# A third of the low weights made by a ScalarE copy and an adding DMA

## The chip, the core and the metric

The kernel runs on one core of a Trainium2 chip. A core has five engines that run side by side, each in the order of its own instruction stream: TensorE (PE in the profile, its weight loads PEld), VectorE (DVE), ScalarE (ACT), GpSimd (POOL) and SyncE (SP), which here only issues DMAs. Engines and DMAs wait for each other by semaphores. The metric is the device time of one execution in microseconds; the time of a kernel is the median of its runs.

## The reference

One layer of a hybrid encoder, for one batch of 256 tokens of width 2048, in float32:

```python
n = rms_norm(h, norm_mix_w[l])
u = n @ w_in[l]
...
mixed = jax.nn.sigmoid(g_attn) * attn_out + jax.nn.sigmoid(g_ssd) * ssd_out
h = h + mixed @ w_out[l]
h = h + conv_ffn(rms_norm(h, norm_ffn_w[l]), ...)
return rms_norm(h, norm_final_w)
```

`attn_out` is a multi-head latent attention with 16 heads, `ssd_out` a chunked state-space scan in both directions with 64 heads in 8 groups, `conv_ffn` a gated MLP of width 5632 with a short convolution. Nearly all the arithmetic lies in products of the 256 tokens with large weight matrices.

## The kernel before

**Split numbers.** The matrix products run in a reduced-precision form of float32 (`F32R`). To keep accuracy, every operand is cut into a high part (the value as rounded to that form) and a low part (the value less its high part), and a product is made of three: high by high, high by low, low by high. The weights come from HBM as float32 and are split on the chip.

**Slabs and halves.** All weights are cut into slabs of 128 x 16 x 128 numbers (1 MB). The list `jobs` holds one entry per slab, in the order in which TensorE multiplies them. A slab lies in one of three `raw` buffers (`RAWB=3`), loaded by SP in `load` (L131 and L133). A slab has two halves, and the list `halves` holds them all: 670, of which 654 have eight blocks of 128 columns and 16, the last ones of the short slabs of `w_dn`, have four. The very first slab is multiplied unsplit and has none.

**The split.** `split_to` takes the halves in order; `hptr[0]` counts them. Each half gets a high buffer `wh` and a low buffer `wl` out of five of each (`HB=5`). ScalarE copies the raw half into `wh` with rounding (L150), and VectorE subtracts the high part from the raw half into `wl` (L151). In the main loop, before the matmuls of half n are emitted, `split_to(n + HB)` emits the split of the halves up to n + 4. The split of half n + 4 takes the buffers that half n - 1 used, so ScalarE waits there for TensorE's last matmul of half n - 1, and TensorE needs the result four halves later. The next load into a `raw` buffer waits for the last reader of that buffer's second half.

**Kinds of jobs.** A dense job (`dense`) multiplies a block of weights `wh` with high and low activations side by side (512 columns, L176) and `wl` with the high activations (256 columns, L177), eight times per half; the last slab of a run uses three matmuls instead (`mm3`, L156 to L158). A quad job (`quad`) has four smaller loads and the weights as the moving side (L204 to L206); it serves the branch gates and the two output projections of the branches. 160 halves belong to quad jobs.

**Stages.** By the trace: latents and the attention up to about 370 us, with quad slabs of the gates and of the attention's output projection in between; the SSD branch from about 395 to 880 us in eight head groups; its output projection, all quad, from 950 to 1126; `w_out` up to 1217; then the FFN up to 1957 in three parts, each an up-projection (`w_up`) with a convolution followed by a down-projection (`w_dn`). In the SSD stage ScalarE and VectorE also carry the convolutions (L672, L675, L676), the decays (`ssd_decay`, L721 to L727) and the scaling of the score blocks (`ssd_p`, L747, L748).

**What sets the order.** The opening block (weights of the first two halves and the first activations) is emitted under `tc.manual_schedule()` and keeps its order. For the rest a planner orders each engine's instructions, with priority in the order of emission; the semaphores follow from which instruction reads and writes which buffer. SP's queue holds nearly all loads in order; ScalarE's queue issues a few small DMAs; GpSimd's queue issues none.

## Time and profile before

| | |
|---|---|
| Median of 3 runs | 1975.71 us (1975.28 to 1976.85) |
| Profiled execution | 1974.66 us |
| Its span, first to last instruction | 1972.9 us |
| TensorE busy | 1956.5 us, 99% |
| VectorE busy | 1466.5 us, 74% |
| ScalarE busy | 1208.5 us, 61% |
| GpSimd busy | 0.2 us |
| DMA traffic | 379.32 MB, mean 192 GB/s |
| Granted TensorE clock, mean | 0.998 |

The page lists the busy time of each engine, the chain of work that ended last, the costliest groups of instructions by line, and the DMA issues. A group row gives line, engine, operation, the tiles it writes and reads, its shape and count, then its busy time, the mean of one in ns, and the engine's idle time just before, with what ended that. A row of waits reads: who waited, for what, us in total, times, longest. A timeline row gives the start in us from the span's begin, the duration, the instruction and, in brackets, the idle time before it and what ended it. A row of a stretch gives its length and each engine's busy time, with counts in brackets. A DMA issue row gives what is written and read, the queue, the count, the size of one and the median time from issue to landing.

### The profile page before, as it was taken

To read this page: it belongs to the slowest core of one execution; us is meant where nothing else is said; L and a number is where in the kernel's file an instruction comes from. 1 tells how busy PE (TensorE), PEld (TensorE's weight loads), DVE (VectorE), ACT (ScalarE), POOL (GpSimd) and SP (SyncE) were. 2 spreads that over 40 slices of the span, in tenths; PEclk is the share of its full clock that TensorE was granted. 3 is DMA by queue.
4 is the path that set the end of the run, shared out by engine and by line. 5 is a ranking of instruction groups with operands and counts; after the bars stand their busy time and mean duration, and the time that the engine had idled before them with its cause. 6 is when DMAs were issued, how large, how long until landed. Compare 5 with 4: busy or idle time off the path is not lost.

```text
span 1972.9 us, 29057 instructions
## 1 busy us (share of the span) xinstructions
PE 1956.5 (99%) x11136; PEld 1702.4 (86%) x11136; DVE 1466.5 (74%) x2349; ACT 1208.5 (61%) x1892; POOL 0.2 (0%) x4
## 2 busy tenths in 40 slices
PE   9999999999999999999999999999999999999997
PEld 8899988888888888888888888888888888888886
DVE  7997745779887988888455576888657777557776
ACT  6666544688988898786444455555435555345564
POOL 0000000000000000000000000000000000000000
PEclk9999999999999999999999999999999999999999
DMA  7554456666466556645766565555555555555553
GB/s 289 166 175 157 137 180 225 230 214 220 165 215 214 204 180 220 221 158 173 229 198 200 199 219 192 188 188 186 185 192 186 180 190 192 179 185 192 187 161 123
DMA packets 93260, 379.32 MB, mean 192 GB/s; under 512 B 10688, under 2 KB 11328, under 8 KB 62912
## 3 DMA queue, kind: packets, MB, share of 16 engines
q1 hardware_dynamic: 91440, 375.09, 56.2%
q10 hardware_dynamic: 1680, 2.37, 0.4%
q8 instruction: 87, 1.43, 0.3%
q14 instruction: 53, 0.43, 0.1%
HBM read 371.91 MB, written 4.33 MB: 191 GB/s over the span
## 4 chain that ended last, share of the span: by engine, by line
PE 93%; DVE 3%; ACT 2%; issue 1%; DMA 1%; SPq 0%; DVEq 0%; ACTq 0%
PE g L176 41%; PE g L177 21%; PE g L204 7%; PE g L206 7%; PE g L205 7%; PE g L158 1%; PE g L157 1%; PE g L156 1%; DVE wl L151 1%; ACT wh L150 1%; PE s L780 1%; PE s L157 0%; PE s L789 0%; DVE bcf L675 0%; PE s L158 0%
## 5 line engine op out<-in xcount | busy, mean ns | idle before, releaser
L151 DVE TENSOR_TENSOR wl<-raw,wh 128x1024 fp32r<-128x1024 f32 (+1 forms) x670 | 809.3, 1212 | 393.9 <-ACT wh L150 381.5
L150 ACT ACTIVATE wh<-raw 128x1024 fp32r<-128x1024 f32 (+1 forms) x670 | 700.3, 1048 | 647.8 <-PE g L176 433.1
L176 PE MATMUL g<-xHL,wh 128*128 128x512 f32 x1424 | 503.7, 398 | 2.0 <-DVE cu L229 2.0
L176 PE MATMUL g<-hHL,wh 128*128 128x512 f32 x1360 | 477.6, 396 | 0.0
L177 PE MATMUL g<-xHL,wl 128*128 128x256 f32 x1424 | 399.8, 281 | 0.8 <-DVE wl L151 0.8
L177 PE MATMUL g<-hHL,wl 128*128 128x256 f32 x1360 | 381.6, 281 | 0.0
L176 PEld LDWEIGHTS g<-xHL,wh 128*128 128x128 f32 x1424 | 267.3, 188 | 65.7 <-issue 1.2
L176 PEld LDWEIGHTS g<-hHL,wh 128*128 128x128 f32 x1360 | 255.1, 188 | 60.8
L177 PEld LDWEIGHTS g<-xHL,wl 128*128 128x128 f32 x1424 | 269.1, 189 | 1.5 <-DVE wl L151 1.1
L177 PEld LDWEIGHTS g<-hHL,wl 128*128 128x128 f32 x1360 | 257.0, 189 | 0.0
L176 PE MATMUL g<-aHL,wh 128*128 128x512 f32 x692 | 243.7, 398 | 0.0
L177 PE MATMUL g<-aHL,wl 128*128 128x256 f32 x692 | 193.2, 280 | 0.0
L176 PEld LDWEIGHTS g<-aHL,wh 128*128 128x128 f32 x692 | 130.0, 188 | 32.1 <-DVE aHL L919 0.7
L177 PEld LDWEIGHTS g<-aHL,wl 128*128 128x128 f32 x692 | 130.5, 189 | 0.1
L204 PE MATMUL g<-wh,xHL 128*128 128x512 f32 x256 | 100.1, 392 | 0.0
L204 PE MATMUL g<-wh,yHL 128*128 128x512 f32 x256 | 99.8, 390 | 0.0
L206 PE MATMUL g<-wh,xHL 128*128 128x512 f32 x256 | 99.8, 390 | 0.0
L205 PE MATMUL g<-wl,xHL 128*128 128x512 f32 x256 | 99.8, 390 | 0.0
L206 PE MATMUL g<-wh,yHL 128*128 128x512 f32 x256 | 99.6, 389 | 0.0
L205 PE MATMUL g<-wl,yHL 128*128 128x512 f32 x256 | 99.6, 389 | 0.0
L901 DVE SCALAR_TENSOR_TENSOR uc<-u,V,uc 128x255 f32<-128x255 f32 x176 | 84.7, 481 | 4.6 <-ACT uc L899 1.5
L176 PE MATMUL g<-mHL,wh 128*128 128x512 f32 x240 | 83.6, 392 | 0.0
(298 smaller groups left out, 2603.5 us busy)
## 6 DMA issues: line engine op xcount, KB each, us to landing
raw<-in_w_in SPq DMA_DIRECT2D x88, 1024.0 KB, 4.9
raw<-in_w_up SPq DMA_DIRECT2D x88, 1024.0 KB, 4.9
raw<-in_w_in SPq DMA_DIRECT2D x128, 256.0 KB, 4.0
raw<-in_w_os SPq DMA_DIRECT2D x128, 256.0 KB, 3.5
raw<-in_w_dn SPq DMA_DIRECT2D x32, 1024.0 KB, 4.9
raw<-in_w_oa SPq DMA_DIRECT2D x64, 256.0 KB, 3.8
FB<-acsD SPq DMA_DIRECT2D x32, 512.0 KB, 7.5
raw<-in_w_out SPq DMA_DIRECT2D x14, 1024.0 KB, 4.9
```

The lines of the kernel that those rows point to most:

```text
L150: act.activation(vh, r, AF.Copy)
L151: dve.tensor_sub(vl, r, f32(vh))
L156: pe.matmul(ps, lhsT=wH, rhs=xH, start=first, stop=False)
L157: pe.matmul(ps, lhsT=wH, rhs=xL, start=False, stop=False)
L158: pe.matmul(ps, lhsT=wL, rhs=xH, start=False, stop=last)
L176: pe.matmul(ps, lhsT=wh[:, b, :], rhs=x, start=k == 0, stop=False)
L177: pe.matmul(ps[:, 0, :], lhsT=wl[:, b, :], rhs=x[:, 0, :], start=False, stop=k == ktot - 1)
L204: pe.matmul(ps, lhsT=x[:, 0, ts], rhs=wH[:, kk, :], start=k == 0, stop=False)
L205: pe.matmul(ps, lhsT=x[:, 0, ts], rhs=wL[:, kk, :], start=False, stop=False)
L206: pe.matmul(ps, lhsT=x[:, 1, ts], rhs=wH[:, kk, :], start=False, stop=k == kt - 1)
L780: pe.matmul(px[j0][:, b, c * P:(c + 1) * P], lhsT=q.xw[:, 1 - c, js], rhs=q.cX[:, 1 - c, :], start=True, stop=True)
L901: dve.scalar_tensor_tensor(o[:, a], u[:, b], vcol("fcw", k * 88 + cb), o[:, a], ALU.mult, ALU.add)
```

## The change

Every third half (`hptr[0] % 3 == 2`), if it has eight blocks and isn't of a quad job, gets its low part in another way: ScalarE copies the raw half a second time, scaled by -1, into `wl`, where the rounding gives the negated high part; then a DMA issued by GpSimd adds the raw half onto it, which leaves raw minus high. The DMA reads the `raw` buffer and `wl` in SBUF and writes `wl`. The other halves keep VectorE's subtraction.

```diff
             act.activation(vh, r, AF.Copy)
-            dve.tensor_sub(vl, r, f32(vh))
+            if hptr[0] % 3 == 2 and nb == 8 and not jobs[i].quad:
+
+                act.activation(vl, r, AF.Copy, scale=-1.0)
+                nc.gpsimd.dma_start(f32(vl), r, accum_op=ALU.add)
+            else:
+                dve.tensor_sub(vl, r, f32(vh))
             hl[hptr[0]] = (wh, wl)
             hptr[0] += 1
```

## The prediction

> **What bounds the kernel now.** I read the page first (busy shares, then the chain that ended last), then TensorE's own list of waits, then the timeline of a quiet stretch, the stretches by time, and the DMA issues.

> ```profile
> span 1972.9 us, 29057 instructions
> PE 1956.5 (99%) x11136; PEld 1702.4 (86%) x11136; DVE 1466.5 (74%) x2349; ACT 1208.5 (61%) x1892; POOL 0.2 (0%) x4
> PE 93%; DVE 3%; ACT 2%; issue 1%; DMA 1%; SPq 0%; DVEq 0%; ACTq 0%
> ```

> TensorE is busy for 1956.5 of 1972.9 us and makes 93% of the chain. VectorE, which the change relieves, stands at 74%, ScalarE, which it loads, at 61%. In the list of waits of TensorE, the largest entry and those for the low weights are:

> ```profile
> PE g L176 <- DVE cu L229: 2.0, 2, 1.1
> PE g L177 <- DVE wl L151: 0.8, 1, 0.8
> PE g L158 <- DVE wl L151: 0.6, 1, 0.6
> ```

> So TensorE waits for the low weights twice in the whole run. What VectorE saves cannot come back as time; the question is only whether the new path keeps the low weights ahead of TensorE. How far ahead they are is read from ScalarE's and TensorE's timelines in the down projection:

> ```profile
> 1704.37 1.06 ACT L150 ACTIVATE wh<-raw 128x1024 fp32r<-128x1024 f32 x1 [1.77 <-PE g L176]
> 1707.20 1.07 ACT L150 ACTIVATE wh<-raw 128x1024 fp32r<-128x1024 f32 x1 [1.77 <-PE g L176]
> 1712.85 1.06 ACT L150 ACTIVATE wh<-raw 128x1024 fp32r<-128x1024 f32 x1 [1.77 <-PE g L176]
> 1712.42 0.40 PE L176 MATMUL g<-aHL,wh 128*128 128x512 f32 x1
> 1712.77 0.40 PE L176 MATMUL g<-aHL,wh 128*128 128x512 f32 x1
> ```

> ScalarE starts a high copy every 2.83 us (1704.37 to 1707.20), each time released by TensorE's last use of the buffer five halves back. With five buffers, TensorE comes to the new half four halves later: 4 x 2.83 = 11.3 us, of which I use 11.2, since ScalarE starts 0.1 us after TensorE has moved on (1712.77 to 1712.85). Today high copy and subtraction take 1.06 + 1.22 us of those 11.2.

> **The change part by part.** Removed: a subtraction on VectorE. Added: a copy on ScalarE and a DMA. Durations by shape, in the groups of instructions:

> ```profile
> L151 DVE TENSOR_TENSOR wl<-raw,wh 128x1024 fp32r<-128x1024 f32 x654 | 798.2, 1225 | 385.0 <-ACT wh L150 372.6 <-DMA raw<-in_w_os 2.1 <-DMA mixS<-mixD 1.5
> L150 ACT ACTIVATE wh<-raw 128x1024 fp32r<-128x1024 f32 x654 | 690.3, 1058 | 636.6 <-PE g L176 422.6 <-PE g L206 169.2 <-PE g L157 16.9
> ```

> How many: of 670 halves 160 belong to quad slabs and 16 are short; of the other 494 the condition takes a third. Counted down the job list it is 166, of which 48 lie in the stretch 395 to 880 us. VectorE loses 166 x 1.225 = 203 us, worth nothing by the waits above. ScalarE gains 166 x 1.058 = 176 us, from 61% to 70%: hidden on the mean, not in every stage.

> The new path from the release of a buffer to its low weights: high copy 1.06, negated copy 1.06, then L, the time from the end of that copy to the DMA's landing. While L is under 11.2 - 2.1 = 9.1 us it is hidden in the quiet stages. The trace has no DMA from the GpSimd queue and none that adds, so L is bounded from the nearest DMA issues (median from issue to landing):

> ```profile
> out<-h ACTq DMA_DIRECT2D x1, 512.0 KB, 2.7
> raw<-in_w_out SPq DMA_DIRECT2D x4, 512.0 KB, 3.6
> raw<-in_w_out SPq DMA_DIRECT2D x14, 1024.0 KB, 4.9
> mixD<-gate SPq DMA_DIRECT2D x4, 512.0 KB, 5.2
> FB<-acsD SPq DMA_DIRECT2D x32, 512.0 KB, 7.5
> CT<-in_cst SPq DMA_DIRECT2D x1, 193.0 KB, 11.3
> q1 hardware_dynamic: 91440, 375.09, 56.2%
> ```

> The lower end is 2.7 us (512 KB out of SBUF on idle queues), the upper 11.3 (the worst that anything waits). The nearest row is the gate's 512 KB out of SBUF beside the weight loads, 5.2 us. An adding DMA must also read what it adds to, so I add what another 512 KB costs a load, 4.9 - 3.6 = 1.3 us: L = 6.5. In throughput the DMAs have room: 91440 packets take 56.2% of the span, and 166 x 128 rows more take 13% if each costs one such packet, 26% if it costs two.

> [...]

> The raw buffer is also held longer. SP's load of the slab after next waits for its last reader, today the subtraction:

> ```profile
> SPq L133 <- DVE wl L151: 1046.3, 215, 8.7
> ```

> Between that half's split and the first split of the new slab lie five halves, 14.1 us. Where the reader becomes the DMA, release and load take 2.1 + 6.5 + 4.9 = 13.5: still in time, by 0.6 us, and that half has the ordinary 9 us of slack behind it. SP waits in order, so the loads behind shift with it; their need is later still. Nothing else stands in the GpSimd queue (4 instructions in all), so a DMA that waits there holds up only the next one, 8.5 us later. I cost all this at nothing; from L = 8 on ScalarE would stand at that load.

> Now the two places where the cover is thin. **The start.** The third half is the first to be added to:

> ```profile
> 17.45 1.06 ACT L150 ACTIVATE wh<-raw 128x1024 fp32r<-128x1024 f32 x1 [0.47 <-DMA raw<-in_w_in]
> 21.56 0.40 PE L176 MATMUL g<-xHL,wh 128*128 128x512 f32 x1
> 21.80 0.28 PE L177 MATMUL g<-xHL,wl 128*128 128x256 f32 x1
> ```

> High copy from 17.45, both copies done at 19.6, landing at 26.1, wanted at 21.8: TensorE stands for 4.3 us. **The SSD stage**, 395 to 880 us, in the stretches by time, with the waits of ScalarE in it:

> ```profile
> 395.00:880.00 485.00, 165.62 (x159) 1.00 0.59 202
> sum 485.00, PE 482.59 PEld 420.84 DVE 415.79 ACT 418.20 POOL 0.00; mean PE 60.32 PEld 52.60 DVE 51.97 ACT 52.27 POOL 0.00
> ACT wh L150 <- PE g L176: 41.4, 42, 1.8
> ACT bcf L676 <- DVE bcf L675: 7.9, 5, 2.1
> ACT sz L701 <- DVE sz L229: 5.3, 8, 1.2
> ```

> (The first row is the high copies alone, the second all work.) ScalarE is busy 418 of 485 us; 48 more copies are 51 us: 469. Of its 67 us idle only the 41 of waiting for TensorE can be filled for certain, so on the mean it wants 469 + 26 = 495, a shortage of 10 us; with the waits for VectorE gone, none. But the work comes in bursts:

> ```profile
> 417.60:449.20 31.60, 31.60 (x209) 27.88 (x208) 23.67 (x40) 30.57 (x53) 0.00 (x0) 1.00 0.54 184
> 484.70:510.30 25.60, 25.60 (x175) 22.68 (x174) 17.42 (x32) 25.20 (x43) 0.00 (x0) 1.00 0.63 208
> 429.12 1.05 ACT L150 ACTIVATE wh<-raw 128x1024 fp32r<-128x1024 f32 x1
> 432.81 1.28 ACT L701 ACT_TABLE_LOAD   x1
> 434.43 1.04 ACT L150 ACTIVATE wh<-raw 128x1024 fp32r<-128x1024 f32 x1
> ```

> In such a stretch ScalarE is busy 30.6 of 31.6 us, and the copies come 5.3 us apart (429.1 to 434.4) where TensorE takes 2.8: 2.5 us late. The stretch has 31.6/2.83 = 11 halves, 3.5 of them adding, so 3.7 us of copies pile up in front of the last. The adding path spares 9.1 - 6.5 = 2.6 us: 2.5 + 3.7 - 2.6 = 3.6 us reach TensorE. Each of the eight head groups has one such stretch: 8 x 3.6 = 29 us. The shortage on the mean is no further term, since TensorE's standing gives ScalarE that time. Bounds: 0 if earlier VectorE results let ScalarE fill its gaps, 51 if every copy is exposed.

> Sum: the profiled execution took 1974.66 us (span 1972.9 and 1.8 around it). 1974.66 + 4.3 + 29 = 2008.0; the median of the runs, 1975.71, stands 1.05 above that execution, so 2009.

> **The rivals.** *The transfer comes later than 9 us.* Then every adding half has TensorE stand L - 9.1 us, in steady state too: the stall at one adding half lengthens the window of the next by as much. For it: 11.3 us above, and two copies of 512 KB and one of 1 MB sharing the DMAs in the same 8.5 us. Against: the like-sized rows lie at 2.7 to 5.8. Price at L = 10: the 118 adding halves outside the SSD stage by 0.9 is 106, the start 7.8, the stage 8 x 7.1 = 57: 2146 us. At 9.3 it is 24 + 7 + 51 = 82: 2058.

> [...]

> [...]

> *Hidden anyway.* L near 3.6 and the gaps of ScalarE filled: the burst comes to 2.5 + 3.7 - 5.5 = 0.7 us, the start to 1.4, so 1983; with L at 2.7 nothing of the burst is left, the start costs 0.5, and it is 1976. For it: the mean load fits if VectorE's waits vanish. Against: ScalarE works 25.2 of 25.6 us from 484.7 on.

> *Faster.* VectorE is in front of TensorE nowhere but in the waits shown; if relief there took all of them and the 2.4 us that TensorE is idle in the SSD stage (485.0 - 482.59), it would give 3.4 + 2.4 = 5.8 us: 1970. It decides only if no adding half is ever late, the third one of the start included, which takes L below 2.2 us, under the lowest row.

> **How the numbers follow.** Forecast, L between 5 and 9 with ScalarE's bursts in front of TensorE: 0.65 (its own range 1995 to 2031, by the same sum). Late transfer: 0.22. Hidden: 0.10, half of it within 0.2% (4 us, about what a measurement of this kernel can tell from no change). Faster: 0.03. Leaving out about 0.1 at either end, the range is 1981 to 2085. Faster 0.03, the same 0.05, slower 0.92.

> **What the profile after would show.** 504 subtractions on L151 and 166 negated copies of 1.06 us on ScalarE; VectorE near 1263 us, ScalarE near 1384; 166 DMAs from the GpSimd queue of 512 KB, landing about 6.5 us after the copy; DMA busy at 70 to 83%. In the list of waits, TensorE waits for that DMA and for high copies, nearly all in the first 30 us and in the stretch 395 to 880, which is some 29 us longer; from 1126 us on TensorE goes on at 2.83 us a half. Waits of 1 us and more spread evenly over the FFN stages would say late transfer; no waits at all, hidden. I would be wrong as well if the planner, which orders ScalarE's work outside the opening block, put it in another order with more or fewer table loads (1.28 us each).

## The result and the profile after

The changed kernel takes 2113.8 us (median; 2109.8 to 2118.1), 1.070 times the kernel before (95% interval 1.0675 to 1.0719): some 138 us more, where the prediction had 33 more and a range that ended at 2085. The profiled execution took 2113.89 us with a span of 2112.1. One run of e2 below, 2136.4 us, lies more than 1.5% above the fastest of its kernel and is left out.

The page of the changed kernel, its head and the chain that ended last (L154 is the adding DMA, L153 the negated copy, L156 the subtraction; the lines behind have moved down by five):

```profile
span 2112.1 us, 29693 instructions
PE 2002.0 (95%) x11136; PEld 1727.2 (82%) x11136; DVE 1281.3 (61%) x2183; ACT 1352.9 (64%) x2052; POOL 143.1 (7%) x170
q0 software_dynamic: 23904, 87.04, 21.8%
PE 55%; DMA 27%; issue 7%; ACT 6%; DVE 4%; SPq 0%; ACTq 0%; POOLq 0%; POOL 0%; DVEq 0%
PE g L181 20%; DMA wl<-raw 16%; PE g L182 10%; PE g L209 6%; PE g L210 6%; PE g L211 6%; DMA raw<-in_w_in 3%; DMA raw<-in_w_up 3%; DMA raw<-in_w_dn 2%; ACT wh L150 2%; DMA FB<-acsD 1%; DVE wl L156 1%; DMA raw<-in_w_out 1%; PE g L162 1%; PE g L163 1%
```

TensorE's share of the chain fell from 93% to 55%, and DMAs rose from 1% to 27%: the adding DMAs (16%) and, behind them, the raw loads (9% by the four rows). VectorE and ScalarE moved the way the sum said, by less (VectorE to 1281 us where 1263 was forecast, ScalarE to 1353 where 1384 was). Two things stand out in TensorE's row: it is idle for 110 us of the span, where it was 16, and it is busy for 45 us more with the same 11136 matmuls.

Who waits, in the changed kernel:

```profile
PEld g L182 <- DMA wl<-raw: 81.1, 49, 4.8
PE g L182 <- DMA wl<-raw: 65.4, 40, 4.4
ACT wh L150 <- DMA raw<-in_w_up: 66.8, 29, 4.4
ACT wh L150 <- DMA raw<-in_w_dn: 46.2, 18, 6.0
ACT FB L729 <- DMA FB<-acsD: 36.0, 7, 9.7
```

TensorE waits for adding DMAs (65 us by the matmuls; the weight loads' 81 us are largely the same waits), but ScalarE's high copies (L150) now wait for raw loads too, 159 us in all, where it was 4.8 before. SP's own list shows why: its loads stand behind adding DMAs.

```profile
SPq L133 <- DMA wl<-raw: 1215.9, 149, 13.0
```

Where the 139 us of the two profiled executions went, with stages cut at TensorE's first matmul of each kind (length before, then the difference to it; the runs e1 to e10 are described below). Each column is one execution: of its kernel's runs it is the quickest in e2, e6 and e9 and the slowest in e1.

| stage | before | after | e1 | e2 | e3 | e4 | e5 | e6 | e7 | e9 | e10 |
|---|---|---|---|---|---|---|---|---|---|---|---|
| start to 365 us | 364.8 | +17.6 | +13.8 | +18.2 | -0.8 | +21.1 | +6.7 | +11.5 | +10.9 | +9.2 | +12.5 |
| SSD and last gates | 585.5 | +59.3 | +70.5 | +50.9 | +9.3 | +52.9 | +15.7 | +22.5 | +37.5 | +11.6 | +24.4 |
| SSD projection (quad) | 176.8 | 0.0 | 0.0 | 0.0 | 0.0 | 0.0 | 0.0 | 0.0 | 0.0 | 0.0 | 0.0 |
| w_out | 90.1 | +8.8 | +6.0 | +2.2 | 0.0 | +4.3 | 0.0 | +2.0 | +1.3 | +1.5 | +1.5 |
| FFN | 743.5 | +52.4 | +30.8 | +52.4 | +0.7 | +28.6 | +0.7 | +1.6 | +1.6 | +1.1 | +1.5 |

(The tail adds at most 1.0.) The stage without adding halves didn't move at all. The others did, the FFN among them, which the prediction had left out.

How late an add is, from the changed kernel's view of the tile `wl` (issue to landing):

```profile
DMA to landing us min/median/max: 4.5/6.7/11.2
```

The median is where the prediction put it, but it isn't one number. By the trace's landings 59 of the 166 take under 5.5 us and 50 over 8.5. The time follows what else the DMA engines carry: between issue and landing the weight loads occupy a DMA engine for 0.7 us in the fast group and 5.9 us in the slow one (medians), and over all adds the two go together with a correlation of 0.94. That is not only because a longer time holds more loads: in the first 4.5 us after the issue, which every add takes, it is 0.4 us in the fast group and 3.9 in the slow one. In the slow group the first row of the add starts 4.8 us after the issue, in the fast one 1.4 us. Between issue and landing of a slow add 219 rows of 8 KB of the weight loads are under way (median), more than the 128 of a whole slab; of a fast one it is 32. Five pairs of buffers leave 9.06 us from the end of the copy until TensorE comes to the half (the prediction's 9.1; below: the window). 43 adds need more than the window, by 49 us in all.

The chain of the changed kernel in the first part of the FFN shows what becomes of that (pieces under 0.1 us left out):

```profile
1451.42 8.51 DMA wl<-raw
1459.99 6.81 DMA raw<-in_w_up
1466.87 2.90 issue
1469.78 10.77 DMA wl<-raw
1480.61 6.33 DMA raw<-in_w_dn
1487.01 2.88 issue
1489.90 10.69 DMA wl<-raw
```

An add of 10.8 us, then the load into the raw buffer that it held, 6.3 us, then 2.9 us until the next add is issued ("issue" is the high and negated copy with what ScalarE does between them), and again: 1469.78 to 1489.90, 20.1 us for three slabs that TensorE multiplies in 17.0 (below: the loop). The FFN does not keep this pace throughout. At 20 us for every three slabs it would lose some 130 us, and it lost 52: adds of 4.5 to 5.5 us that meet hardly any load stand in between.

### The profile page after: what moved, and what is told of

Its sections match the earlier page's. It is cut to its first block, busy times and chain, and to the rows that moved or that the text cites. A ratio compares the mean times of both kernels' runs of the same rounds, so it can differ in the third digit from the quotient of the medians.

```text
span 2112.1 us, 29693 instructions
## 1 busy us (share of the span) xinstructions
PE 2002.0 (95%) x11136; PEld 1727.2 (82%) x11136; DVE 1281.3 (61%) x2183; ACT 1352.9 (64%) x2052; POOL 143.1 (7%) x170
## 3 DMA queue, kind: packets, MB, share of 16 engines
q1 hardware_dynamic: 91440, 375.09, 52.1%
q0 software_dynamic: 23904, 87.04, 21.8%
## 4 chain that ended last, share of the span: by engine, by line
PE 55%; DMA 27%; issue 7%; ACT 6%; DVE 4%; SPq 0%; ACTq 0%; POOLq 0%; POOL 0%; DVEq 0%
PE g L181 20%; DMA wl<-raw 16%; PE g L182 10%; PE g L209 6%; PE g L210 6%; PE g L211 6%; DMA raw<-in_w_in 3%; DMA raw<-in_w_up 3%; DMA raw<-in_w_dn 2%; ACT wh L150 2%; DMA FB<-acsD 1%; DVE wl L156 1%; DMA raw<-in_w_out 1%; PE g L162 1%; PE g L163 1%
## 5 line engine op out<-in xcount | busy, mean ns | idle before, releaser
L150 ACT ACTIVATE wh<-raw 128x1024 fp32r<-128x1024 f32 (+1 forms) x670 | 699.1, 1046 | 590.1 <-PE g L181 225.5
L156 DVE TENSOR_TENSOR wl<-raw,wh 128x1024 fp32r<-128x1024 f32 (+1 forms) x504 | 607.7, 1207 | 485.2 <-ACT wh L150 480.2
L181 PE MATMUL g<-xHL,wh 128*128 128x512 f32 x1424 | 517.9, 406 | 11.1 <-DVE sz L234 6.2
L181 PE MATMUL g<-hHL,wh 128*128 128x512 f32 x1360 | 484.8, 400 | 0.0
L182 PE MATMUL g<-xHL,wl 128*128 128x256 f32 x1424 | 407.6, 286 | 29.2 <-DMA wl<-raw 28.1
L182 PE MATMUL g<-hHL,wl 128*128 128x256 f32 x1360 | 388.0, 285 | 27.2 <-DMA wl<-raw 27.1
L181 PEld LDWEIGHTS g<-xHL,wh 128*128 128x128 f32 x1424 | 274.4, 193 | 77.2 <-DVE sz L234 7.2
L182 PEld LDWEIGHTS g<-xHL,wl 128*128 128x128 f32 x1424 | 276.2, 194 | 36.1 <-DMA wl<-raw 34.0
L182 PEld LDWEIGHTS g<-hHL,wl 128*128 128x128 f32 x1360 | 261.8, 192 | 33.9 <-DMA wl<-raw 33.8
L154 POOL DMA_DIRECT2D wl<-raw x166 | 142.9, 861 | 1945.9 <-ACT wl L153 1041.7
L153 ACT ACTIVATE wl<-raw 128x1024 fp32r<-128x1024 f32 x166 | 173.7, 1046 | 5.0 <-PE g L210 3.1
## 6 DMA issues: line engine op xcount, KB each, us to landing
raw<-in_w_in SPq DMA_DIRECT2D x88, 1024.0 KB, 5.8
raw<-in_w_up SPq DMA_DIRECT2D x88, 1024.0 KB, 5.8
wl<-raw POOLq DMA_DIRECT2D x166, 512.0 KB, 6.7
raw<-in_w_dn SPq DMA_DIRECT2D x32, 1024.0 KB, 6.8
FB<-acsD SPq DMA_DIRECT2D x32, 512.0 KB, 10.1
```

The source lines that it names most:

```text
L150: act.activation(vh, r, AF.Copy)
L153: act.activation(vl, r, AF.Copy, scale=-1.0)
L154: nc.gpsimd.dma_start(f32(vl), r, accum_op=ALU.add)
L156: dve.tensor_sub(vl, r, f32(vh))
L181: pe.matmul(ps, lhsT=wh[:, b, :], rhs=x, start=k == 0, stop=False)
L182: pe.matmul(ps[:, 0, :], lhsT=wl[:, b, :], rhs=x[:, 0, :], start=False, stop=k == ktot - 1)
```

## The experiments

Each ratio is to the kernel before, run beside it.

**e1: a fourth raw buffer.** It gives the loop of the raw buffers a third more time.

```diff
-RAWB=3, HB=5, NPG=29, NP1=18
+RAWB=4, HB=5, NPG=28, NP1=17
```

> The changed kernel with a fourth raw buffer, paid for with one page and one small page fewer. Loop theory: with three buffers a raw buffer goes load, copies, adding DMA, load, some 20 us round where three slabs take 17; a fourth buffer gives it 22.6 us, so the FFN and w_out stages (some 62 us of the 138 lost) come back to 2.83 us a half and the time falls to 2010 to 2050. Window theory: the adding DMA simply lands after more than the 9 us that five pairs of weight buffers leave; a raw buffer more changes nothing, 2100 to 2125. Traffic theory: the DMAs are too full, again no change.

Measured: 2091.3 us, ratio 1.0586 (1.0566 to 1.0606). The loop theory expected 2010 to 2050, and the others no change: neither is right alone. The FFN lost 30.8 instead of 52.4 us, and ScalarE's waits for `w_up` loads are gone from its list, but TensorE's waits for the adds are not:

```profile
PEld g L182 <- DMA wl<-raw: 64.2, 39, 6.1
PE g L182 <- DMA wl<-raw: 51.6, 32, 5.8
```

**e2: a sixth pair of weight buffers.** It gives every low half 2.8 us more.

```diff
-RAWB=3, HB=5, NPG=29, NP1=18
+RAWB=3, HB=6, NPG=28, NP1=17
```

> The changed kernel with six pairs of weight buffers instead of five, and one page and one small page fewer. Window theory: 2.8 us more for every low half, enough for all but the slowest adds, so 2010 to 2050. Loop theory: the loop of the raw buffers does not pass through these, at 20 us for three slabs it still sets the pace: 2085 to 2120.

Measured: 2108.6 us (mean of three runs, 2099.1 to 2125.4), ratio 1.0673 (1.0606 to 1.0739): as the loop theory said, no gain that stands out of the spread of its runs. The wait moved to the raw loads, which is the loop seen from ScalarE; its largest such wait in this run (66.8 us in the changed kernel):

```profile
ACT wh L150 <- DMA raw<-in_w_up: 137.1, 41, 6.8
```

**e3: the ScalarE copies alone.**

```diff
                 act.activation(vl, r, AF.Copy, scale=-1.0)
-                nc.gpsimd.dma_start(f32(vl), r, accum_op=ALU.add)
+                dve.tensor_sub(vl, r, f32(vh))
```

> Each adding half gets the negated ScalarE copy, and then VectorE's subtraction over it as before; no DMA. What ScalarE's 166 extra copies cost by themselves. By the prediction's reading ScalarE runs out of slack in the bursts of the SSD stage: 1985 to 2010, all of the growth in the SSD stage. If the DMA alone is at fault: 1974 to 1980.

Measured: 1984.6 us, ratio 1.0044 (1.0029 to 1.0059). The growth is in the SSD stage alone, as expected, but it is 9.3 us and not 29. Its stretch of that stage, beside the same of the kernel before:

```profile
365.00:960.00 595.00, 585.81 (x3451) 507.90 (x3450) 497.87 (x898) 522.53 (x882) 0.00 (x0) 1.00 0.58 197
```

```profile
365.00:950.00 585.00, 582.59 (x3448) 506.42 (x3448) 496.39 (x898) 485.53 (x836) 0.00 (x0) 1.00 0.59 200
```

ScalarE (fourth of the pairs of time and count) gained 37 us, where the 52 extra copies of this longer stretch take 54. Of the difference 10 us are 8 table loads fewer (8 x 1.28; 56 in the whole run instead of 64): the planner put its work in another order. It does so in every run, with 54 to 64 table loads, so a difference of some 10 us between two runs in this stage can be the order's. What the copies cost in the old order isn't shown. With the subtraction so soon after the copy, the window's slack stays large here; this run doesn't tell what the bursts cost when the add uses the slack up.

**e4: the DMA adds a tile that stays.** The copies and the DMA's way into the low half are kept; it doesn't read the raw half and so doesn't hold it.

```diff
+    still = cp.tile([P, 8, P], F32, name="still")
+    dve.memset(still, 0.0)
...
-                nc.gpsimd.dma_start(f32(vl), r, accum_op=ALU.add)
+                nc.gpsimd.dma_start(f32(vl), still, accum_op=ALU.add)
```

> The same copies and adding DMAs onto the low half, but the DMA adds a tile of zeros that stays in SBUF instead of the raw half, so that it does not hold the raw buffer (the low half is then the negated copy, left at that); one small page fewer. Loop theory: the FFN and w_out stages return to 2.83 us a half, 2010 to 2050. Window or traffic theory: the DMA is as long as before and the time stays at 2090 to 2120.

Measured: 2081.5 us, ratio 1.0545 (1.0493 to 1.0597): better, and outside both ranges, like e1. The FFN's loss is 28.6 us. The adds themselves are later, 8.6 us in the median:

```profile
wl<-still POOLq DMA_DIRECT2D x166, 512.0 KB, 8.6
```

86 of them now take over 8.5 us from issue to landing. Without the hold the raw loads aren't kept back, and more of them run beside an add: 4.5 us of load between its issue and its landing on the mean, where the changed kernel has 3.0. The loop had been spacing the two.

**e5: a quarter of the add.**

```diff
-                nc.gpsimd.dma_start(f32(vl), r, accum_op=ALU.add)
+                nc.gpsimd.dma_start(f32(vl[:, :2, :]), r[:, :2, :], accum_op=ALU.add)
```

> The changed kernel, but the DMA adds only the first two of the eight blocks (128 KB of 512; in the other six the low half stays the negated copy). One add's own rows then take 0.7 us of a DMA engine instead of 2.6, and the loads lose a quarter as much to it. If the size of the transfer is what is late: landing 4 to 6 us after the copy's end, nearly all under 9, and 1985 to 2010, the 9 us that the copies alone cost and little more. If it is the queueing behind a raw load and the round trip, which do not depend on its size: landings of 7 to 9 us stay where a load is in front, and 2020 to 2070.

Measured: 1998.0 us, ratio 1.0113 (1.0098 to 1.0128), inside the first range. 29 of the 166 still take over 5.5 us, behind a load, but only one exceeds the window:

```profile
wl<-raw POOLq DMA_DIRECT2D x166, 128.0 KB, 3.1
q0 software_dynamic: 23904, 21.77, 7.4%
```

w_out and FFN are back at their old length (+0.7 us). Queue and round trip are not what is late; the 512 KB are. (A 1 KB row of this add takes 109 ns of a DMA engine, which is a third, and not a quarter, of a 4 KB row's 328.)

**e6: a plain copy instead of the add.**

```diff
-                nc.gpsimd.dma_start(f32(vl), r, accum_op=ALU.add)
+                nc.gpsimd.dma_start(f32(vl), r)
```

> The changed kernel with a plain copying DMA of the same 512 KB from the same queue in place of the adding one (the low half is then the raw half itself). The price of adding: in the changed kernel a 4 KB row of the add takes 327 ns of a DMA engine. If a plain row takes half of that, landings are 1.3 us shorter when alone and some 2 to 3 us shorter beside a load, and the time is 2010 to 2060; if the price lies in the queue and not in the addition, 2095 to 2120.

Measured: 2017.3 us, ratio 1.0212 (1.0192 to 1.0232), inside the first range. Same queue, same bytes, same holds and waits; 96 us of the 138 are gone. A 4 KB row takes 159 ns of a DMA engine instead of 328 (medians of 21248 rows each), and the issues land earlier:

```profile
q0 software_dynamic: 23904, 87.04, 10.9%
wl<-raw POOLq DMA_DIRECT2D x166, 512.0 KB, 4.7
DMA to landing us min/median/max: 2.8/4.7/9.7
```

Nine of them exceed the window, against 43 of the adds. This is the run that shows where most of the loss came from: the doubled engine time of adding, through window and loop.

**e7 and e8: both buffers at once, and their price.** e7 is the changed kernel, e8 the kernel before, with the same line:

```diff
-RAWB=3, HB=5, NPG=29, NP1=18
+RAWB=4, HB=6, NPG=28, NP1=9
```

> The changed kernel with a fourth raw buffer and a sixth pair of weight buffers at once, paid for with one page and half of the small pages (to be held against the next run). If loop and window are two ways in which the same late landings reach TensorE, and each hides behind the other: w_out and FFN lose less than 10 us, and the time against the next run is plus 30 to 70, nearly all in the SSD stage. If something else bounds these stages: plus 100 or more.

> The kernel before with the same buffers as the run just described (four raw, six pairs, 28 pages, 9 small pages). No low half is late in the kernel before, so more weight buffers give it nothing: 1972 to 1980 if the pages suffice; anything above is the price of the missing pages.

Measured: e7 2026.6 us, ratio 1.0256 (1.0241 to 1.0272); e8 1974.2, ratio 0.9995 (0.9986 to 1.0005), so the missing pages cost nothing. e7 against e8 is plus 52 us, as expected. The fourth raw buffer alone brought 23 us, the sixth pair alone 5, which is less than the spread of its runs, both together 87. In e7 the adds are no quicker than in the changed kernel, but few are still waited for:

```profile
DMA to landing us min/median/max: 4.5/7.5/12.3
PE g L182 <- DMA wl<-raw: 9.3, 4, 5.7
```

w_out and FFN lose 2.9 us in all. So the loss of these stages (61 us) is the same late landings, reaching TensorE by two ways, of which each takes over when the other is opened.

**e9: the adds beside the old path.** VectorE subtracts as before; the DMAs add onto two spare tiles.

```diff
+    spare = [cp.tile([P, 8, P], F32, name=f"spare{_}") for _ in range(2)]
+    for t in spare:
+        dve.memset(t, 0.0)
...
-                act.activation(vl, r, AF.Copy, scale=-1.0)
-                nc.gpsimd.dma_start(f32(vl), r, accum_op=ALU.add)
+                dve.tensor_sub(vl, r, f32(vh))
+                nc.gpsimd.dma_start(spare[hptr[0] // 3 % 2], r, accum_op=ALU.add)
```

> Every low half is subtracted on VectorE as before; the 166 adding DMAs run beside it, from the raw half onto two spare tiles that nobody reads (one page and one small page fewer, no extra ScalarE copy). Traffic and the hold on the raw buffer without the wait for the low half. If the adds hurt by slowing the weight loads: 2000 or more, with TensorE or ScalarE waiting for raw loads. If they hurt only where their own landing is waited for: within 10 us of the kernel before, 1972 to 1986; the DMA starts as soon as the half has landed, so load and add, 6 + 10 us, still fit into the 17 of three slabs.

Measured: 2006.2 us, ratio 1.0154 (1.0137 to 1.0171); the profiled execution is the quickest of four, 1998.5. A miss for the second theory, which had at most 1986, and half a hit for the first: the growth lies at the start and in the SSD stage (+9.2 and +11.6 us of the table), where ScalarE waits for loads that the traffic and the held buffers make late:

```profile
ACT wh L153 <- DMA raw<-in_w_in: 14.2, 10, 3.9
ACT FB L732 <- DMA FB<-acsD: 13.7, 7, 4.5
```

The other three runs take some 8 us more than the profiled one; in which stage isn't shown. In w_out and FFN, traffic and hold cost 2.6 us when nobody waits for the landing and the add starts as soon as the half is there.

**e10: e7 with the FB loads on GpSimd's queue.**

```diff
-                nc.sync.dma_start(st[c], acsD[c:c + 1, r0:r0 + 8, :].broadcast_to([P, 8, P]))
+                nc.gpsimd.dma_start(st[c], acsD[c:c + 1, r0:r0 + 8, :].broadcast_to([P, 8, P]))
```

> The kernel with four raw buffers and six pairs, and the 32 loads of the decay rows FB moved from SP's queue to GpSimd's. In that kernel's SSD stage, 37 us longer than before, ScalarE stands 30 us for these loads (3 us in the kernel before) and TensorE hardly ever for an add. If they are late because SP serves in order and stands at raw loads that an add holds: the wait falls under 10 us, the stage is 15 to 25 longer and the time 2000 to 2016. If they are late only because the DMAs are shared with the adds: no change, 2020 to 2035.

Measured: 2016.1 us, ratio 1.0201 (1.0181 to 1.0221), just above the first range; the wait did not fall as far as expected. ScalarE's wait for these rows in the stretch 380 to 1000 us, first in e7, then here, and their landing here:

```profile
ACT FB L729 <- DMA FB<-acsD: 30.3, 6, 8.9
```

```profile
ACT FB L729 <- DMA FB<-acsD: 20.3, 4, 8.5
FB<-acsD POOLq DMA_DIRECT2D x32, 512.0 KB, 12.0
```

Off SP's queue the stage is 13 us shorter, so SP's order is part of it; but the loads themselves are late as well: from issue to landing they take 7.5 us in the kernel before, 10.7 in e7 in the same queue of SP, and 12.0 here. Here an add can also stand in front of them in GpSimd's queue, so how much is due to the shared DMA engines and how much to that queue isn't told apart.

## Why the prediction was wrong

**What bounds the kernel, and the worth of the relief: right.** VectorE fell by 185 us (203 were forecast) and nothing came back. In no run that adds was any stage more than 1 us shorter.

**Where the sum fell short.** The stages lost 105 us more than the sum had: w_out and FFN 61, which it had at nothing, the SSD stage 59 instead of 29, and the stretch up to 365 us 17.6 instead of 4.3.

**L = 6.5: right as a median, wrong as a number to work with.** Issue to landing is 6.7 in the median and 4.5 to 11.2 in its ends; the range stated for L (2.7 to 11.3) held, but the sum took one value for all 166 against a window of 9.1. That the median came out is partly luck, since it lies between two groups, alone and beside a load, and the forecast had only one. With a quarter of the adds over the window, the FFN couldn't be free. The price of adding was taken as a second read of 1.3 us. No run shows such a read by itself; what they show is that a 4 KB row of an add takes 328 ns where a plain one (e6) takes 159, so 8 rows for each of 16 engines take 2.6 us instead of 1.3: that size was right for an add alone. What the sum left out is that load and add delay each other: the 50 slow adds, beside the most load, take 8.5 to 11.2 us, those beside next to none 4.5 in the median; and the 1 MB loads of `w_in`, `w_up`, `w_dn` and `w_out`, 4.9 us from issue to landing in the kernel before, take 5.8, 5.8, 6.8 and 7.0 (medians).

**The step that failed: "release and load take 2.1 + 6.5 + 4.9 = 13.5: still in time, by 0.6 us", and then "I cost all this at nothing".** It looked at one leg, from the split of one slab to the first split of the next, and found 0.6 us to spare. It is a closed loop. In the FFN two adds come in every six halves, at the same places in three slabs, and there are three raw buffers, so the same two buffers carry every add, and a load that comes late makes the next add late. The loop's time is load + copies + add: by the predicted sizes 4.9 + 2.1 + 6.5 = 13.5 of 17.0 us, by those of the chain shown above 6.3 + 2.9 + 10.8 = 20.0. So to see the loop would not have been enough: with sizes taken from transfers that do not meet it still fits, by 3.5 us, and what failed is to put at nothing a path whose parts slow each other. The margin of 0.6 us was the warning, and the price "from L = 8 on ScalarE would stand at that load" named the mechanism with no sum behind it. e2 against e7 shows what the loop costs when the window is wide enough (82 us of time), e1 against e7 what the window costs when the loop is (65 us).

**The late-transfer rival** had its mechanism right, and its price for L = 10 (2146) is near the result, but L is not 10 for all. 43 adds are over the window, by 49 us in sum, a third of the loss. Of the 65 us for which TensorE waits for adds, 47 are for 30 of these 43; the other 18 are for ten adds that were within the window, so by the same count their copies came late. The rest of the loss has to come from elsewhere: other waits, most of them in the SSD stage, and the clock (below).

**ScalarE's bursts in the SSD stage: too large for the copies, too small for the stage.** The 29 us were measured at 9.3 for the copies alone (e3). The stage's 59 us come from elsewhere too: with 1/4 of the add 15.7, with a plain copy 22.5, with both buffers 37.5 us. The queue of SP, which holds the FB loads, was costed at nothing in the same sentence ("the loads behind shift with it; their need is later still"); ScalarE waits for them 36 us in the changed kernel, and e10 gains by taking them out of that queue. TensorE's own waits in the stretch 380 to 1020 us of the changed kernel show both kinds, 23.6 us for adds and some 18 for results of ScalarE and VectorE:

```profile
PE g L182 <- DMA wl<-raw: 23.6, 13, 3.7
PE g L181 <- DVE sz L234: 6.2, 2, 5.0
PE g L181 <- DVE cu L234: 4.5, 3, 1.8
PE s L161 <- ACT bcH L688: 4.4, 3, 3.6
```

How far ScalarE's and VectorE's lag there comes from the copies, from the FB loads or from late raw loads stays open.

**The start: right at the third half, partly by luck.** 4.3 us were forecast there. TensorE's timeline of the changed kernel:

```profile
27.64 0.58 PE L182 MATMUL g<-xHL,wl 128*128 128x256 f32 x1 [4.45 <-DMA wl<-raw]
```

The add landed 1.5 us later than forecast (27.6 instead of 26.1 us), and TensorE came to it 1.4 us later as well (23.2 instead of 21.8), so the difference came out. The other 13 us up to 365 us had no term: TensorE waits there 2.4 and 1.7 us for split latents and 2.5 us for split queries and keys, and some 7 us go to the clock (below).

**Issue to landing without the loads: 4.5 us.** The GpSimd instruction takes 0.86 us in 162 of the 166 cases, and the time to landing follows the weight loads. The measured median of a plain copy (e6) is 4.7 us and that of an add 6.7, both beside loads. The copies and adds beside which next to no load ran (under 0.2 us of a DMA engine) take 2.9 and 4.5 in the median.

## What to carry to other kernels

A transfer that takes over the work of an engine also takes over its place in the recycling of buffers: sum the whole loop (load, compute, transfer, and back to the load) against the time in which the consumer uses up as many buffers as there are, with durations as they are when the parts overlap (here 20.0 us by the chain, where sizes from transfers that do not meet gave 13.5, against 17.0). Where two buffers bound the same path, opening one shows little (here 23 and 5 us of time, both together 87); open both before saying that buffers don't matter.

## What was not expected of the hardware

In the changed kernel TensorE loses more by many of its waits than the wait itself. Windows of the changed kernel around one (columns: window, length, then busy time with count of PE, PEld, DVE, ACT and POOL, then the granted clock, DMA share and GB/s):

```profile
1493.20:1496.60 3.40, 3.40 (x21) 2.95 (x20) 0.00 (x0) 0.97 (x2) 0.00 (x0) 1.00 0.97 290
1496.60:1500.40 3.80, 1.12 (x7) 0.74 (x6) 2.95 (x5) 2.58 (x5) 0.00 (x0) 1.00 0.78 219
1500.40:1503.80 3.40, 3.40 (x11) 2.92 (x12) 2.06 (x3) 1.37 (x2) 0.86 (x1) 0.50 0.65 149
1503.80:1507.20 3.40, 3.40 (x21) 2.96 (x21) 0.95 (x1) 1.06 (x1) 0.00 (x0) 0.99 0.99 252
```
